# SSD output and its gate with channels on partitions in a fused two-layer decoder kernel

## The chip, the cores and the metric

The kernel runs as one program on one core of a Trainium2 chip. The metric is device time in microseconds (us) of one launch. The kernel before took 1224.19 us as the median of three runs (1223.19 to 1224.21). The engines are named as in the profile: PE is TensorE (matrix products; PEld its weight loads), DVE is VectorE, ACT is ScalarE, POOL is GpSimd, SP is SyncE, which here only issues transfers.

## What is computed

Two layers over a sequence of 256 tokens of width 2048. Layer 0 is a Mamba-2 mixer, layer 1 a dilated attention that the change doesn't touch. Cut to what matters here, with 8 groups of 8 heads of 64 channels each:

```python
proj = h @ in_w                          # 2048 -> z (4096), x/B/C (6144), dt (64)
z, xBC, dt = split(proj)
xs, Bm, Cm = split(silu(conv(xBC)))      # xs 4096, Bm and Cm 8 x 128
acum  = cumsum(dt * A)                   # per head, over the 256 tokens
decay = exp(acum[l] - acum[s])           # causal
y  = (Cm @ Bm.T * decay) @ (xs * dt)     # per head; the kernel goes in blocks of 128 tokens
y  = y + xs * D_skip
y  = y * silu(z)
y  = y * rsqrt(mean(y**2 over the 512 channels of a group) + eps) * norm_g
x  = layer_norm(alpha * x + (1 + gate) * (y @ out_w))
```

Tokens 128 to 255 take a part from the first 128 tokens through a state (`po` in the kernel: Cm times the state), scaled by exp(acum), and each block has its own part (`py`).

## The kernel before

**Products in two parts.** Every weight piece of 128x1024 f32 is loaded by SP's queue, then split: ACT copies it to a rounded type (`whi`, L100), DVE subtracts to get the rest (`wlo`, L102). A product is the sum of hi x hi, lo x hi and hi x lo, so each piece costs one ACT pass, one DVE pass and three passes on PE. A product of one group can be made with the channels on partitions (`cm_quad`: the weight is stationary, 12 matmuls of 128x256 for each 128 rows of the contraction) or with tokens on partitions (`tm_chunk`: the activations are stationary, 6 matmuls of 128x512).

**Order.** Instructions are placed on each engine by a scheduler that goes by modelled times; `issue_after` pins one instruction behind another, and `background` pops jobs from a list (columns of the adaptive gates, 128x2048 on DVE, L317) at a rate of so many for each piece. Each engine then works its list strictly in order.

**The mixer's loop.** For each group g the kernel makes B and C, xs and z of the next group while it works on this one. `scores` makes Cm x Bm. `stage1` makes the decay matrices `seg` on ACT and DVE (from `cbc`, the cumulative sums, loaded by broadcast), transposes xs to tokens on partitions (L776), and makes `xd` (times dt), the product with D (into y, L781, DVE) and `xo`. `stage2` makes `po` (one 128x512 matmul, L798), `py` (32 matmuls of 64x64, L809, whose halves go to different halves of the output partitions), adds, multiplies by silu(z), and takes sums of squares with ACT's accumulator (L812). y has tokens on partitions, so a root is one number for each partition. `stage3` scales by the root (ACT, L820).

**The output projection.** `y_tiles(g)` turns y around: eight transposes on PE (L864), and for each of four channel tiles one ACT pass (hi, L868) and one DVE pass (lo, L869), both of 128x256 from PSUM. y(0) is turned during the last z product (z of group 7), y(1) to y(7) during the first of four column groups of the output projection (`wout`, n = 0 to 3, 16 pieces each), two pieces for each y. Column group n is closed by `residual` (DVE), which takes the gate's row by a broadcast.

## Time and profile before

| what | value |
|---|---|
| median of three runs | 1224.19 us (1223.19 to 1224.21) |
| the profiled execution's own time | 1223.81 us |
| its span | 1222.0 us |
| mean granted TensorE clock | 0.999 of full speed |
| busy: PE, DVE, ACT | 1208.8, 1019.6, 703.9 us |
| stages touched by the change | the mixer's loop, about 180 to 511 us, and the first column group of the output projection, up to about 562 us |

Busy times count what an engine executes. Matmuls overlap in PE's pipeline, so a matmul of 128x512 is shown with about 392 ns though one is started about every 227 ns; how often something starts is what a row's place in time, or a run of many in the chain of waits, shows. DVE instructions overlap a little in the same way: the row's duration is longer than the time to the next start.

### The profile page before, as it was taken

To read this page: it belongs to the slowest core of one execution; us is meant where nothing else is said; L and a number is where in the kernel's file an instruction comes from. 1 tells how busy PE (TensorE), PEld (TensorE's weight loads), DVE (VectorE), ACT (ScalarE), POOL (GpSimd) and SP (SyncE) were. 2 spreads that over 40 slices of the span, in tenths; PEclk is the share of its full clock that TensorE was granted. 3 is DMA by queue.
4 is the path that set the end of the run, shared out by engine and by line. 5 is a ranking of instruction groups with operands and counts; after the bars stand their busy time and mean duration, and the time that the engine had idled before them with its cause. 6 is when DMAs were issued, how large, how long until landed. Compare 5 with 4: busy or idle time off the path is not lost.

```text
span 1222.0 us, 19072 instructions
## 1 busy us (share of the span) xinstructions
PE 1208.8 (99%) x7244; PEld 1039.5 (85%) x7244; DVE 1019.6 (83%) x1450; ACT 703.9 (58%) x1057; POOL 3.9 (0%) x8
## 2 busy tenths in 40 slices
...
GB/s 374 421 421 423 422 264 239 259 327 224 230 190 194 182 173 207 226 327 334 370 317 298 211 203 342 350 344 379 385 376 280 281 261 174 113 193 160 193 260 69
DMA packets 81372, 335.94 MB, mean 275 GB/s; under 512 B 9200, under 2 KB 9984, under 8 KB 68480
## 3 DMA queue, kind: packets, MB, share of 16 engines
...
q0 software_dynamic: 576, 1.05, 0.6%
...
q14 instruction: 35, 0.29, 0.1%
q10 hardware_dynamic: 208, 0.08, 0.0%
...
## 4 chain that ended last, share of the span: by engine, by line
PE 77%; DVE 13%; ACT 5%; DMA 3%; issue 2%; DVEq 0%; ACTq 0%
PE acc L224 25%; PE acc L190 21%; PE acc L193 11%; DVE wlo L102 4%; DVE araw L317 4%; PE acc L233 3%; PE acc L234 3%; PE acc L232 3%; DMA raw<-in_win 3%; ACT whi L100 2%; DVE cacc L391 2%; PE acc L151 1%; PE acc L153 1%; PE acc L152 1%; PE py L809 1%
## 5 line engine op out<-in xcount | busy, mean ns | idle before, releaser
L100 ACT ACTIVATE whi<-raw 128x1024 fp32r<-128x1024 f32 x389 | 408.2, 1057 | 329.5 <-PE acc L190 107.1
L102 DVE TENSOR_TENSOR wlo<-raw,whi 128x1024 fp32r<-128x1024 f32 x389 | 470.2, 1221 | 128.3 <-ACT whi L100 121.1
L190 PE MATMUL acc<-actT,whi 128*128 128x512 f32 x1280 | 401.7, 394 | 0.5 <-DVE xs L202 0.5
L193 PEld LDWEIGHTS acc<-actT,wlo 128*128 128x128 f32 x1280 | 239.6, 188 | 52.3 <-DVE wlo L102 0.7
L193 PE MATMUL acc<-actT,wlo 128*128 128x256 f32 x1280 | 255.2, 281 | 0.3 <-DVE wlo L102 0.3
L317 DVE SCALAR_TENSOR_TENSOR araw<-araw,cb__72 128x2048 f32<-128x2048 f32 x95 | 217.0, 2284 | 3.2 <-DMA araw<-in_ada 3.0
L190 PEld LDWEIGHTS acc<-actT,whi 128*128 128x128 f32 x1280 | 195.0, 188 | 1.7 <-DVE xs L202 0.9
L224 PE MATMUL acc<-whi,actT 128*128 128x512 f32 x560 | 144.5, 392 | 0.5 <-ACT whi L100 0.5
L224 PEld LDWEIGHTS acc<-whi,actT 128*128 128x128 f32 x560 | 104.2, 188 | 22.0 <-ACT whi L100 0.9
L233 PE MATMUL acc<-wlo,actT 128*128 128x512 f32 x272 | 106.8, 393 | 2.2 <-DVE wlo L102 2.1
L232 PE MATMUL acc<-whi,actT 128*128 128x512 f32 x272 | 105.0, 394 | 0.2 <-ACT sz L664 0.2
L151 PE MATMUL acc<-actT,whi 128*128 128x256 f32 x372 | 103.5, 281 | 1.0 <-ACT sz L664 0.5
L224 PE MATMUL acc<-wlo,actT 128*128 128x512 f32 x384 | 103.6, 391 | 0.0
L153 PE MATMUL acc<-actT,wlo 128*128 128x256 f32 x372 | 101.9, 281 | 1.5 <-DVE wlo L102 1.5
L152 PE MATMUL acc<-actT,whi 128*128 128x256 f32 x372 | 103.0, 279 | 0.0
L234 PE MATMUL acc<-whi,actT 128*128 128x512 f32 x256 | 100.0, 391 | 0.0
L224 PEld LDWEIGHTS acc<-wlo,actT 128*128 128x128 f32 x384 | 71.7, 188 | 14.4
L151 PEld LDWEIGHTS acc<-actT,whi 128*128 128x128 f32 x372 | 69.6, 188 | 2.6 <-ACT sz L664 0.9
L153 PEld LDWEIGHTS acc<-actT,wlo 128*128 128x128 f32 x372 | 68.9, 188 | 2.3 <-DVE wlo L102 2.3
L152 PEld LDWEIGHTS acc<-actT,whi 128*128 128x128 f32 x372 | 70.6, 190 | 0.2
L233 PEld LDWEIGHTS acc<-wlo,actT 128*128 128x128 f32 x272 | 51.1, 188 | 13.8 <-DVE wlo L102 3.7
L232 PEld LDWEIGHTS acc<-whi,actT 128*128 128x128 f32 x272 | 50.9, 188 | 10.5 <-ACT sz L664 0.6
...
## 6 DMA issues: line engine op xcount, KB each, us to landing
...
raw<-in_win SPq DMA_DIRECT2D x109, 512.0 KB, 6.0
raw<-in_wout SPq DMA_DIRECT2D x64, 512.0 KB, 5.7
raw<-in_wbin SPq DMA_DIRECT2D x64, 512.0 KB, 4.1
raw<-in_wxs SPq DMA_DIRECT2D x48, 512.0 KB, 4.5
raw<-in_wv SPq DMA_DIRECT2D x48, 512.0 KB, 6.7
raw<-in_wk SPq DMA_DIRECT2D x48, 512.0 KB, 7.6
cbc<-cumd SPq DMA_DIRECT2D x16, 512.0 KB, 5.1
```

The costliest lines, as they stand in the source:

```text
L100: copied.append(S.activation(hi, raw, AF.Copy))
L102: latest.append(V.tensor_tensor(lo, raw, hi.bitcast(F32), op=ALU.subtract))
L151: T.matmul(o, hi[:, k, c_], ahi[:, kt, :], start=first, stop=False, skip_group_check=True)
L152: T.matmul(o, hi[:, k, c_], alo[:, kt, :], start=False, stop=False, skip_group_check=True)
L153: T.matmul(o, lo[:, k, c_], ahi[:, kt, :], start=False, stop=kt == k1 - 1, skip_group_check=True)
L190: T.matmul(ps[n], hi[:, k, n * P:n * P + P], both(kt), start=kt == 0, stop=False, skip_group_check=True)
L193: T.matmul(ps[n][:, 0, :], lo[:, k, n * P:n * P + P], high(kt), start=False, stop=kt == KT - 1, skip_group_check=True)
L224: T.matmul(ps[b], a_(kt)[:, b * P:b * P + P], w_[:, k, :], start=a_ is ahi and w_ is hi and kt == k0, stop=w_ is lo and kt == k1 - 1)
L232: T.matmul(o, h_, hi[:, k, :], start=kt == k0, stop=False, skip_group_check=part)
L233: T.matmul(o, h_, lo[:, k, :], start=False, stop=False, skip_group_check=part)
L234: end = T.matmul(o, l_, hi[:, k, :], start=False, stop=kt == k1 - 1, skip_group_check=part)
L317: return V.scalar_tensor_tensor(raw, raw, 1.0, cb_, op0=ALU.mult, op1=ALU.mult, accum_out=mod[layer][:, ct, j:j + 1])
```

## The change

**z and y with channels on partitions.** z is now made by `cm_quad`, and y[g] holds four channel tiles of 128 channels by 256 tokens. `py` takes xd as the stationary operand and `seg` as the moving one: 16 matmuls with 64 weight columns and 128 moving columns each, the even heads to the lower and the odd heads to the upper half of the output partitions. `po` is four matmuls of 128x128.

**What a token-wise factor becomes.** A factor for each token is now a factor along a row. exp(acum) for `po` is made by four ACT passes of 64x256 (`grow`) in `stage1`. The product with D is a factor for each partition: four ACT passes of 128x256 instead of two DVE passes of 128x512. The mean of squares goes over partitions: ACT squares y (128x1024), DVE adds the four channel tiles in two instructions (128x512, 128x256), and PE multiplies the sum by a column of ones (two matmuls of one column). The roots go through DRAM: GpSimd's queue (POOL) writes them to `rootd` and loads them back as a broadcast over all partitions (128x256 for groups 0 and 1, one 128x1024 for groups 2 to 5, 128x256 each for 6 and 7).

**Turning y.** No transposes: DVE multiplies by norm_g and the root (`y_scale`, four passes of 128x256 out of SBUF), then one ACT pass and one DVE pass of 128x1024 split y (`y_split`).

**Order of the projection.** Column group 0 goes over its pieces 0 to 13 (y(1) to y(6) are scaled and split there, `stage3` of group 7 at piece 1), then column group 1 over its pieces 0 to 13 (y(7) at its piece 2), then pieces 14 and 15 of both, each followed by its `residual`. The rates of the background jobs change from (1, 2) and (1, 4) to (1, 3) and (2, 5).

```diff
             def stage1(g, cb):
-                segs = []
+                segs, grow = [], px.tile([P, 4, P], F32, name="grow", bufs=1)
...
+                    for n, rows_ in enumerate((slice(0, 64), slice(64, 128))):
+                        S.activation(grow[rows_, 2 * w:2 * w + 2, :], cbc[rows_, n:4:2, 1, :], AF.Exp)
...
-                    V.tensor_tensor(y[g][:, b, :].rearrange("p (h e) -> p h e", h=HPG), heads,
-                                    dskip[:, g * HPG:(g + 1) * HPG, None].to_broadcast([P, HPG, 64]),
-                                    op=ALU.mult)
...
+                for i in range(4):
+                    S.activation(y[g][:, i, :], xs[g][:, i, :], AF.Copy, scale=pv("dsk")[:, 4 * g + i:4 * g + i + 1])
...
-            def stage2(g, segs, xd, cb, xo):
+            def stage2(g, segs, xd, cb, xo, grow):
...
-                T.matmul(po, cb[:, 2, :], xo, start=True, stop=True)
...
-                behind = z_end[-1] if g in (0, 4, 7) else None
+                behind = z_end[-1] if g in (0,2,3,4,7) else None
+                for i in range(4):
+                    c_ = slice(i * P, i * P + P)
+                    with tc.issue_after(behind.ins) if behind is not None else ExitStack():
+                        behind = T.matmul(po[:, c_], xo[:, c_], cb[:, 2, :], start=True, stop=True)
+                xo = xo.rearrange("p (i n) -> p i n", i=4)
+                V.tensor_tensor(xo, po.rearrange("p (i n) -> p i n", i=4), grow, op=ALU.mult)
+                V.tensor_tensor(y[g][:, :, P:], xo, y[g][:, :, P:], op=ALU.add)
...
-                                T.matmul(py[t_, e_], segs[hh // 4][:, hh % 4, b, t_], xd[:, b, e_], start=True, stop=True)
+                                behind = T.matmul(py[t_, hh // 2, b * P:b * P + P], xd[:, b, 64 * h:64 * h + 64],
+                                         segs[w][:, hh, b, :], start=True, stop=True)
...
+                V.tensor_tensor(y[g], y[g], sz[g], op=ALU.mult)
+                sq = sz[g]
+                S.activation(sq, y[g], AF.Square)
+                return sq
-            def stage3(g, rs):
+            def stage3(g, sq):
-                for b in range(2):
-                    S.activation(y[g][:, b, :], y[g][:, b, :], AF.Copy, scale=rs[:, b:b + 1])
+                V.tensor_tensor(sq[:, 0:2, :], sq[:, 0:2, :], sq[:, 2:4, :], op=ALU.add)
+                sums = sq[:, 0, :]
+                V.tensor_tensor(sums, sums, sq[:, 1, :], op=ALU.add)
+                ss = (aux if g == G - 1 else aux2).tile([P, 512], F32, name="aux" if g == G - 1 else "py")[:, :2]
+                for b in range(2):
+                    T.matmul(ss[:, b:b + 1], sums[:, b * P:b * P + P], ones[:, 0:1], start=True, stop=True)
...
+                nc.gpsimd.dma_start(rootd[g * L:g * L + L].rearrange("(b p) -> p b", p=P), rsqrt(ms, "a"))
...
+            def y_scale(g):
+                if g < 2:
+                    roots[g] = p0.tile([P, L], F32, name="cacc", bufs=3)
+                    bcast(roots[g], rootd, g * L, queue=PO)
+                elif g in (2, 6):
+                    t = slots.tile([P, 4, L], F32, name=f"s{g // 6}")
+                    roots.update({g + j: t[:, j, :] for j in range(min(4, G - g))})
+                    n = min(4, G - 1 - g)
+                    bcast(t[:, :n, :].rearrange("p i l -> p (i l)"), rootd, g * L, queue=PO)
+                elif g == G - 1:
+                    bcast(roots[g], rootd, g * L, queue=PO)
+                for i in range(4):
+                    V.scalar_tensor_tensor(y[g][:, i, :], y[g][:, i, :], pv("normg")[:, 4 * g + i:4 * g + i + 1],
+                                           roots[g], op0=ALU.mult, op1=ALU.mult)
+            def y_split(g):
+                val = y[g].rearrange("p i (j r) -> p i r j", r=2)
+                hi, lo = (t.rearrange("p i (r j) -> p i r j", r=2) for t in y_to(g))
+                S.activation(hi, val, AF.Copy)
+                V.tensor_tensor(lo, val, hi.bitcast(F32), op=ALU.subtract)
             def y_tiles(g):
-                        T.transpose(pt[:, i % 2, b * P:b * P + P], y[g][:, b, i * P:i * P + P], ident)
...
-                    S.activation(hi, by_parity, AF.Copy, scale=w)
-                    V.scalar_tensor_tensor(lo, by_parity, w, hi.bitcast(F32), op0=ALU.mult, op1=ALU.subtract)
+                if g > 1:
+                    y_scale(g)
+                y_split(g)
...
         def y_ahead(q):
-            if q % 2 == 0 and q // 2 + 1 < G:
+            if q == 1:
+                with tc.high_priority():
+                    stage3(G - 1, rs)
+            if q % 2 == 0 and q // 2 + 1 < G - 1:
                 y_tiles(q // 2 + 1)
...
+        out_pieces(0, 0, KT - 2, y_ahead)
+        out_pieces(1, 0, KT - 2, lambda q: y_tiles(G - 1) if q == 2 else None)
+        drain()
...
+        for n in range(2):
+            out_pieces(n, KT - 2, KT)
+            joined(n, pss[n])
```

Three places of the order show how the scheduler lays this out. In them `s_94` to `s_101` are y(0) to y(7), `sz` the gate of a group and later its squares, `acc` an accumulator, `actT` the activations of the product (later the hi part of y), `xs` at these places the two parts of y(0), `ylo` the lo part of y(1) to y(7) in turn.

PE where the last z product ends and the output projection begins, first before, then with the change:

```order
2336 L234 MATMUL acc<-whi,actT 128x512
2337 L798 MATMUL aux<-xo,cb 128x512
2338 L809 MATMUL py<-xd,seg 64x64 x32
2339 L864 MATMUL aux<-cc,s_95 128x128 x4
2340 L224 MATMUL acc<-whi,xs 128x512 x8
2341 L224 MATMUL acc<-wlo,xs 128x512 x4
2342 L224 MATMUL acc<-whi,xs 128x512 x2
2343 L864 MATMUL aux<-cc,s_95 128x128 x2
```

```order
3108 L153 MATMUL acc<-actT,wlo 128x256
3109 L791 MATMUL aux<-cb,xo 128x128 x4
3110 L802 MATMUL py<-seg,xd 64x128 x16
3111 L228 MATMUL acc<-wlo,xs 128x512 x4
3112 L228 MATMUL acc<-whi,xs 128x512 x8
3113 L228 MATMUL acc<-wlo,xs 128x512 x4
3114 L228 MATMUL acc<-whi,actT 128x512 x4
3115 L818 MATMUL aux<-cc,sz 128x1 x2
3116 L228 MATMUL acc<-whi,ylo_6270 128x512 x4
```

The transposes are gone; the sum over partitions for group 7 (L818) now stands on PE between the twentieth matmul of the projection and the first that reads the lo part of y(1).

DVE at the same boundary, before and with the change:

```order
563 L102 TENSOR_TENSOR wlo<-raw,whi 128x1024 x2
564 L799 TENSOR_TENSOR xo<-aux,dec 128x512
565 L801 TENSOR_TENSOR s_101<-xo,s_101 128x512
566 L810 TENSOR_TENSOR s_101<-py,s_101 128x512
567 L102 TENSOR_TENSOR wlo<-raw,whi 128x1024
568 L811 TENSOR_TENSOR s_101<-s_101,sz 128x512
569 L810 TENSOR_TENSOR s_101<-py,s_101 128x512
570 L811 TENSOR_TENSOR s_101<-s_101,sz 128x512
571 L869 SCALAR_TENSOR_TENSOR ylo_5568<-aux,prm,actT 128x256 x2
```

```order
574 L794 TENSOR_TENSOR s_101<-xo,s_101 128x4x128
575 L871 SCALAR_TENSOR_TENSOR s_98<-s_98,prm,s_6350 128x256
576 L805 TENSOR_TENSOR s_101<-py,s_101 128x512 x2
577 L871 SCALAR_TENSOR_TENSOR s_98<-s_98,prm,s_6350 128x256
578 L806 TENSOR_TENSOR s_101<-s_101,sz 128x1024
579 L102 TENSOR_TENSOR wlo<-raw,whi 128x1024 x2
580 L813 TENSOR_TENSOR sz<-sz 128x512
581 L871 SCALAR_TENSOR_TENSOR s_98<-s_98,prm,s_6350 128x256
582 L815 TENSOR_TENSOR sz<-sz 128x256
583 L871 SCALAR_TENSOR_TENSOR s_99<-s_99,prm,s_6350 128x256
584 L820 TENSOR_SCALAR ms<-aux 128x2
585 L879 TENSOR_TENSOR ylo_6270<-s_95,actT 128x1024
```

With the change the scalings of y(2) to y(4) and one of y(5) stand ahead of the first lo part that the projection needs, and that lo part stands behind the mean of squares of group 7 (L820), which reads what L818 leaves.

DVE a little earlier, where the broadcast roots of groups 2 to 5 (`s_6350`, in the place of y(0)) are first read; this is new, and before there is nothing in its place:

```order
565 L102 TENSOR_TENSOR wlo<-raw,whi 128x1024 x3
566 L871 SCALAR_TENSOR_TENSOR s_96<-s_96,prm,s_6350 128x256
567 L102 TENSOR_TENSOR wlo<-raw,whi 128x1024
568 L871 SCALAR_TENSOR_TENSOR s_96<-s_96,prm,s_6350 128x256 x3
569 L102 TENSOR_TENSOR wlo<-raw,whi 128x1024
570 L871 SCALAR_TENSOR_TENSOR s_97<-s_97,prm,s_6350 128x256 x4
571 L102 TENSOR_TENSOR wlo<-raw,whi 128x1024
572 L793 TENSOR_TENSOR xo<-aux,grow 128x512
```

The first scaling of y(2) waits for that broadcast, and weight pieces of the last z product (L102) stand behind it.

155 lines of the change are left out of this document (72 added, 83 removed).

## The prediction

> **What bounds the kernel now.** First the page: engines, and the chain that ended last.
>
> ```profile
> span 1222.0 us, 19072 instructions
> PE 1208.8 (99%) x7244; PEld 1039.5 (85%) x7244; DVE 1019.6 (83%) x1450; ACT 703.9 (58%) x1057; POOL 3.9 (0%) x8
> PE 77%; DVE 13%; ACT 5%; DMA 3%; issue 2%; DVEq 0%; ACTq 0%
> ```
>
> PE is busy nearly all the time, and three quarters of the chain is its work, so a matmul that goes away is worth its time, unless another engine is just behind. Whether one is must be read by stage. The windows (busy time of PE, PEld, DVE, ACT; then granted clock, DMA share, GB/s):
>
> ```profile
> 180.00:222.00 42.00, 41.55 (x258) 36.85 (x257) 31.33 (x55) 33.46 (x55) 0.00 (x0) 1.00 0.72 250
> 222.00:301.00 79.00, 77.20 (x570) 67.05 (x569) 79.00 (x127) 58.10 (x99) 0.00 (x0) 1.00 0.75 263
> 380.00:470.00 90.00, 90.00 (x673) 77.99 (x672) 83.58 (x153) 79.62 (x145) 0.00 (x0) 1.00 0.61 198
> 470.00:511.00 41.00, 40.30 (x306) 33.06 (x304) 36.02 (x72) 32.88 (x57) 0.00 (x0) 1.00 0.54 187
> 511.00:562.00 51.00, 51.00 (x252) 41.46 (x252) 49.40 (x77) 30.47 (x50) 0.00 (x0) 1.00 0.85 314
> ```
>
> The clock is 1.00 in all of them. From 470 to 562 us, the last z product and the turning of y, DVE has 85.4 of 92 us: 6.6 us of room. That is where the change adds DVE work. In the loop before it, DVE is full from 222 to 301 us, and ACT has 79.6 of 90 us from 380 to 470.
>
> Then the pace of each kind of instruction, from runs of equals in the chain of waits (start, us, engine and line, count):
>
> ```profile
> 405.92 0.87 PE aux L776 x8
> 451.31 2.36 DVE cacc L391 x6
> 459.00 3.40 DVE wlo L102 x3
> 508.03 0.86 PE aux L798 x2
> 508.89 2.02 PE py L809 x64
> 561.67 119.72 PE acc L224 x528
> ```
>
> So PE takes 119.72/528 = 0.227 us for 512 columns (half of it, 0.113, for 256) and 0.109 for a transpose. `po` counts two passes and `py` 64, since these f32 products go through PE twice: 0.86 and 2.02 us a group, 0.84 ns a column. DVE takes 1.13 us for 128x1024 and 0.39 for a 256-wide operation with a scalar. The timeline of DVE (start, duration) gives the others, and DVE's rest in the last z product:
>
> ```profile
> 488.41 0.69 DVE L811 TENSOR_TENSOR s<-s,sz 128x512 f32<-128x512 f32 x1
> 489.02 0.42 DVE L750 TENSOR_TENSOR cb<-aux,cc 128x256 f32<-128x256 f32 x1
> 489.35 0.29 DVE L751 COPY cb<-aux 128x128 f32<-128x128 f32 x1
> 490.69 0.16 DVE L814 TENSOR_SCALAR ms<-ss 128x2 f32<-128x2 f32 x1
> 490.76 0.69 DVE L778 TENSOR_TENSOR xd<-aux,dtT 128x512 f32<-128x512 f32 x1
> 503.77 1.23 DVE L102 TENSOR_TENSOR wlo<-raw,whi 128x1024 fp32r<-128x1024 f32 x1 [0.50 <-ACT whi L100]
> 506.49 1.23 DVE L102 TENSOR_TENSOR wlo<-raw,whi 128x1024 fp32r<-128x1024 f32 x1 [1.49 <-ACT whi L100]
> 508.93 0.69 DVE L799 TENSOR_TENSOR xo<-aux,dec 128x512 f32<-128x512 f32 x1 [1.21 <-PE aux L798]
> ```
>
> From start to start: 0.61 us for 128x512, 0.33 for a plain 256-wide one, 0.07 for 128x2. In brackets stand 3.2 us in which DVE waited.
>
> **The change part by part.**
>
> z costs PE the same either way: 12 x 0.113 against 6 x 0.227 us for 128 rows of the contraction. The gate's ACT and DVE work keeps its size. Nothing here.
>
> *Transposes of y.* 64 go. Bare, by the pace above, 64 x 0.109 = 7.0 us. In the first column group they stand singly among matmuls; the timeline of PE has the first and the last of 56 of them:
>
> ```profile
> 510.83 0.66 PE L864 MATMUL aux<-cc,s 128*128 128x128 f32 x4
> 554.54 0.38 PE L864 MATMUL aux<-cc,s 128*128 128x128 f32 x2
> ```
>
> By the order of the kernel before, 54 transposes and 163 matmuls of 512 columns lie between these starts: 43.71 - 163 x 0.227 = 6.7 us, 0.124 each, 8.0 for 64. I take -7.5 (-7.0 to -8.0).
>
> *py.* Before, 64 passes of 64 columns take 2.02 us, 31 ns each, where 64 columns at 0.84 ns are 54: the two halves of the output partitions run side by side. Now 32 passes of 128 columns, 107 ns alone. Side by side in the same proportion they take 1.9 us a group (-0.15, over eight groups -1.2); perfectly, 1.7 (-2.3); one behind the other 3.4 (+11.4). Before, both halves read the same moving data and now they read different data. The rows of the second layer's halves are the nearest:
>
> ```profile
> L1162 PE MATMUL aux<-s,q x96: 221/222/271, 1028.1 to 1137.6; 128*64 128x64 f32 x96
> ```
>
> They have the same 222 ns of latency as L809's, which speaks for side by side. I take -1.2.
>
> *po.* Four matmuls of 128 columns for one of 512, same columns: +0.04 us a group for three more starts, +0.3 (0 to +0.8).
>
> *Sums over partitions.* Two one-column matmuls a group, four passes with a full weight load, 32 in all; no row has one. Between 31 ns (L809's pass) and 109 (L776's): 1.0 to 3.5 us. The load is a full one, but it can overlap; I take the middle, +2.0.
>
> *The loop, groups 0 to 6.* DVE loses two 128x512 products with D (1.22 us) and gains the two adds of the squares (0.61 + 0.39); the small rest leaves about -0.3 a group. ACT changes more. Its rows in the last z product:
>
> ```profile
> L868 ACT ACTIVATE actT<-aux,prm 128x256 fp32r<-128x256 f32 x28 | 12.3, 468 | 9.0 <-PE aux L864 9.0
> L820 ACT ACTIVATE s<-s,ay 128x512 f32<-128x512 f32 x6 | 4.0, 715 | 1.1 <-DVE ay L281 1.1
> L765 ACT ACTIVATE seg<-cbc,cumT 128x128 f32<-128x128 f32 x16 | 5.1, 387 | 0.0
> ```
>
> The product with D costs 4 x 0.47, `grow` about 4 x 0.4 to 0.47, the two scalings (2 x 0.72) go: about +1.8 us a group. From 380 to 470 us ACT has 10.4 us of room for some three groups, 3.5 each: hidden, with half the cover used up; without it, 1.8 a group. PE's own rest from 180 to 301 us is 0.45 + 1.8 = 2.3 us, which DVE's relief could take away. I take -0.5 (-2.3 to +2).
>
> *The stretch where y is finished.* I follow DVE's order from the mean of squares of group 5 to the lo part of y(1), and PE's from the sums (L818) of group 5 to the first matmul that reads that lo part; DVE cannot start before PE's sums, nor PE pass the end before DVE. DVE has 17 of 128x1024 (11 are lo parts of weights), 16 of 128x512, 32 of about 128x256, 24 of 128x2 and a copy: 17 x 1.13 + 16 x 0.61 + 32 x 0.39 + 24 x 0.07 + 0.2 = 43.4 us. PE has 192 z matmuls of 256 columns (21.8), 28 of the projection (6.3), 16 transposes (1.7), scores (0.6), two `po` and two `py` (1.7 + 3.8) and four one-column matmuls (0.4): 36.3 us, with about 1 for switching. So PE must wait 6 to 7 us somewhere in it, however early DVE's inputs come. The cause is what the rearrangement puts on DVE there: the lo parts of y cost 0.4 x 4 from PSUM before; now the scaling costs that, and the split 1.13 on top, for each y. The products with D, which left DVE, were spread over the loop.
>
> The order puts the largest part of it at the end. Behind the last z product PE has `po` and `py` (2.8 us) and 20 matmuls (4.5), then the sums of group 7. They wait for DVE's eight operations from the `po` product to the multiply by silu(z) (4.8 us), ACT's square, two lo parts and the adds: 9.4 us behind z's end at the least, 2.1 after PE is there, and the lo part of y(1) 1.3 later. With DVE already late by some 3 us, of which z's own pieces take part, I get 8.5 in all by hand. I take +7.3 (6 to 8.5). The kernel before's own rest in this stretch, 0.7 us by the window from 470 to 511, is part of that and comes off: -0.7.
>
> *The broadcast roots.* POOL's queue can load the roots of groups 2 to 5 only when y(0)'s split has freed its place; four lo parts, one scaling and a few tiny ones later, 5.3 us by DVE's pace, DVE wants them, and three weight pieces of z stand behind it. The rows of such transfers (time to landing), and of an issue on POOL:
>
> ```profile
> cbc<-cumd SPq DMA_DIRECT2D x16, 512.0 KB, 5.1
> L1350 POOL DMA_DIRECT2D out<-u x4: 996/1287/1558, 1207.2 to 1209.5; - x4
> DMA to landing us min/median/max: 4.2/8.1/8.6
> ```
>
> By the broadcast of the same size on SP, 5.1 us, the roots are just in time; with the issue of 1.3 and POOL's slowest landing of 8.6 they are 4.6 late, a lateness that goes straight into DVE's sum. I take 0 (0 to +4.6), since the nearest row is the one of the same pattern and size.
>
> *The projection behind it.* After the lo part of y(1), DVE has 1.13 us of split, 1.6 of scaling and about two weight pieces for each y, while PE has 24 matmuls (5.4 us) for it, so DVE gets ahead again. The joining of column groups 0 and 1 moves back by 28 pieces together, so the gate's row has more time. 0.
>
> Sum: -7.5 - 1.2 + 0.3 + 2.0 - 0.5 + 7.3 - 0.7 = -0.3 on the profiled 1223.81, 1223.5; the median of the runs is 0.4 above the profiled execution, so **1223.9 us**: no change that a measurement can tell (0.2%, 2.4 us, is about what one of this kernel can).
>
> [...]
>
> **Rivals.**
>
> *PE's saving shows.* If the scalings out of SBUF start every 0.33 us, as the plain 256-wide row L750 does, the 32 operations of that width give 1.9 us back; if the loop's relief takes away PE's 2.3 us of rest; and with transposes at -8.0: -0.3 - 1.9 - 1.8 - 0.5 = -4.5, or 1219.7; with sums at 1.0 and `py` at -2.3, 1217.6. I call it 1218.5. For it: L391's six run in dependent pairs, so its 0.39 may hold a wait, and DVE is full from 222 to 301 us. Against it: L869, a scaling of the same form out of PSUM, has 0.40 too, and PE's rests there come from weight pieces.
>
> *The roots come late.* The mechanism above, slower: with POOL's landing at its median of 8.1 us and the issue of 1.3 they are 4.1 late, 1228.0; with the hand count of 8.5 on the boundary, 1229.2. It decides from a landing of about 5.3 us after the split. For it: the median of POOL's rows is above; against it: those are stores at the end of the kernel, in competition with SP's.
>
> *The halves of py run one behind the other.* +12.6 against my term: 1236.5, less what DVE's lateness in the last two groups hides (1.6 each at most), about 1234. For it: different moving data in the halves. Against: the latency of L1162. [...]
>
> **Chances.** Forecast (within 0.2%) 0.37; PE's saving shows 0.35; the roots or the boundary later than I count 0.20; halves in sequence 0.08. So faster by over 0.2% 0.35, within it 0.37, slower 0.28. The forecast's own range is 1221.8 to 1226.6, the bounds of no change. The whole one reaches to the lower end of the first rival and a little past the second's hand count: 1217 to 1230.
>
> **What would show it.** `po`, `py` as grouped runs: 0.9 and 1.9 us (3.4 would be the third rival). No rows at all of L864's kind. PE's waits in the last z product and the first twenty matmuls of the projection: 6 to 8.5 us in sum, released by DVE's `wlo` and `ylo`; under 4 would be the first rival. At the first scaling of y(2), DVE waiting on a DMA by over 1 us would be the second. The scalings' pace, 0.39 or 0.33. The forecast is wrong if PE's waits in the loop grow by over 2 us (ACT's cover gone), or if the join of column groups 0 and 1 waits.

## The result

The changed kernel takes **1236.88 us** (median of six runs, 1235.23 to 1240.34) where the kernel before takes 1224.20 (1223.19 to 1225.40): a ratio of 1.0109, 95% interval 1.0092 to 1.0126. It is 12.7 us slower. The forecast was 1223.9 us with a range of 1217 to 1230; the result lies outside it, on the side that had a chance of 0.28. Among the kernels further down, one execution of burst_earlier is left out, which took 1495.92 us at a granted clock of 0.753.

The profiled execution took 1240.34 us, 3.5 more than its kernel's median, so what is read from the trace below adds up to more than 12.7 us. The first lines of the page, and the chain of waits by engine:

```profile
span 1238.5 us, 20144 instructions
PE 1210.6 (98%) x7772; PEld 1074.9 (87%) x7772; DVE 1026.3 (83%) x1450; ACT 711.5 (57%) x1056; POOL 12.5 (1%) x21
PE 73%; DVE 11%; ACT 7%; DMA 6%; issue 3%; SPq 0%; DVEq 0%; ACTq 0%
```

PE is busy 1.8 us longer than before in a span 16.5 us longer, though it has less to do, and the chain runs through ACT and DMA more often (7% and 6% against 5% and 3%). Work has left PE, and waiting has come in.

### The profile page after: what moved, and what is told of

It is laid out like the page before. It is cut to its first block, busy times and chain, and to the rows that moved or that the text cites. A ratio compares the mean times of both kernels' runs of the same rounds, so it can differ in the third digit from the quotient of the medians.

```text
span 1238.5 us, 20144 instructions
## 1 busy us (share of the span) xinstructions
PE 1210.6 (98%) x7772; PEld 1074.9 (87%) x7772; DVE 1026.3 (83%) x1450; ACT 711.5 (57%) x1056; POOL 12.5 (1%) x21
## 4 chain that ended last, share of the span: by engine, by line
PE 73%; DVE 11%; ACT 7%; DMA 6%; issue 3%; SPq 0%; DVEq 0%; ACTq 0%
PE acc L228 23%; PE acc L194 21%; PE acc L197 11%; DMA raw<-in_win 3%; DVE wlo L102 3%; DVE araw L320 3%; PE acc L153 3%; PE acc L151 3%; PE acc L152 3%; ACT whi L100 2%; DVE cacc L392 2%; DMA araw<-in_ada 2%; ACT seg L757 1%; PE py L802 1%; PE acc L238 1%
## 5 line engine op out<-in xcount | busy, mean ns | idle before, releaser
L102 DVE TENSOR_TENSOR wlo<-raw,whi 128x1024 fp32r<-128x1024 f32 x389 | 470.2, 1221 | 135.9 <-ACT whi L100 130.5
L197 PEld LDWEIGHTS acc<-actT,wlo 128*128 128x128 f32 x1280 | 239.5, 188 | 54.5 <-DVE wlo L102 2.3
L197 PE MATMUL acc<-actT,wlo 128*128 128x256 f32 x1280 | 254.8, 280 | 1.5 <-DVE wlo L102 1.3
L153 PE MATMUL acc<-actT,wlo 128*128 128x256 f32 x884 | 242.1, 279 | 7.9 <-DVE wlo L102 7.9
L151 PE MATMUL acc<-actT,whi 128*128 128x256 f32 x884 | 245.4, 280 | 1.3 <-ACT whi L100 0.7
L152 PE MATMUL acc<-actT,whi 128*128 128x256 f32 x884 | 244.6, 278 | 0.0
L194 PEld LDWEIGHTS acc<-actT,whi 128*128 128x128 f32 x1280 | 194.8, 188 | 0.6
L153 PEld LDWEIGHTS acc<-actT,wlo 128*128 128x128 f32 x884 | 164.8, 189 | 10.1 <-DVE wlo L102 9.9
L151 PEld LDWEIGHTS acc<-actT,whi 128*128 128x128 f32 x884 | 166.9, 189 | 2.9 <-ACT whi L100 0.9
L152 PEld LDWEIGHTS acc<-actT,whi 128*128 128x128 f32 x884 | 166.9, 189 | 0.2 <-issue 0.2
L228 PE MATMUL acc<-whi,actT 128*128 128x512 f32 x560 | 144.4, 392 | 0.5 <-ACT whi L100 0.5
L228 PEld LDWEIGHTS acc<-whi,actT 128*128 128x128 f32 x560 | 105.1, 189 | 23.0 <-ACT whi L100 0.9
L228 PE MATMUL acc<-wlo,actT 128*128 128x512 f32 x384 | 104.1, 393 | 0.0
L228 PEld LDWEIGHTS acc<-wlo,actT 128*128 128x128 f32 x384 | 72.7, 189 | 16.0
L228 PE MATMUL acc<-whi,ylo 128*128 128x512 f32 x208 | 57.4, 399 | 1.4 <-DVE ylo L879 1.4
L757 ACT ACTIVATE seg<-cbc,cumT 128x128 f32<-128x128 f32 x128 | 40.9, 388 | 5.1 <-PE py L802 3.4
```

Of the source, the lines that this page charges most:

```text
L102: latest.append(V.tensor_tensor(lo, raw, hi.bitcast(F32), op=ALU.subtract))
L151: T.matmul(o, hi[:, k, c_], ahi[:, kt, :], start=first, stop=False, skip_group_check=True)
L152: T.matmul(o, hi[:, k, c_], alo[:, kt, :], start=False, stop=False, skip_group_check=True)
L153: end = T.matmul(o, lo[:, k, c_], ahi[:, kt, :], start=False, stop=kt == k1 - 1, skip_group_check=True)
L194: T.matmul(ps[n], hi[:, k, n * P:n * P + P], both(kt), start=kt == 0, stop=False, skip_group_check=True)
L197: T.matmul(ps[n][:, 0, :], lo[:, k, n * P:n * P + P], high(kt), start=False, stop=kt == KT - 1, skip_group_check=True)
```

## The profile after, and where the time went

I went through PE's list in the trace from 180 us to the first matmul of layer 1 and gave each matmul its steady pace (0.227 us for 512 columns, 0.113 for 256, 59 ns for a pass of the new `py`, 31 for one of the old, and so on); what lies between two starts beyond that is counted as lost. The marks are starts of state products (`po`).

| stretch of PE's list | before: work, lost (us) | after: work, lost (us) |
|---|---|---|
| 180 us to the sixth state product (452.5 / 459.7 us) | 265.0, 7.6 | 264.7, 14.9 |
| sixth to eighth state product (507.9 / 519.6 us) | 52.7, 2.7 | 54.0, 6.0 |
| eighth to the first matmul of layer 1 (692.9 / 708.5 us) | 181.6, 3.5 | 175.9, 12.9 |
| sum | 499.3, 13.8 | 494.6, 33.8 |

So 4.7 us of work are saved and 20.0 us more are lost: +15.3 at the end of the mixer (15.5 by the marks; the table is good to some 0.2 us). Layer 1 adds another 0.9 to the profiled span's matmuls and is not followed here. The loss stands at three places: the loop (+7.3), the last z product (+3.3) and the start of the output projection (+9.4).

**The loop.** The windows (busy time of PE, PEld, DVE, ACT, POOL; then granted clock, DMA share, GB/s), in three of the stretches that were shown of before:

```profile
222.00:301.00 79.00, 74.47 (x582) 69.95 (x581) 75.95 (x119) 58.17 (x98) 0.87 (x1) 0.98 0.71 251
380.00:470.00 90.00, 90.00 (x679) 82.83 (x678) 81.47 (x150) 78.70 (x140) 2.17 (x3) 1.00 0.71 173
...
511.00:562.00 51.00, 44.01 (x242) 37.24 (x241) 46.38 (x70) 23.03 (x23) 2.54 (x4) 0.90 0.84 236
```

From 380 to 470 us, where I feared for ACT's room, PE still has 90 of 90. The loss in the loop is earlier: from 222 to 301 us PE is busy for 74.47 us, before for 77.20, and the granted clock has fallen under 1. The other one is at the boundary, 511 to 562 us, where PE had 51 of 51 and now has 44.01, at a clock of 0.90. PE's longest waits, summed over the run (us in total, times, longest):

```profile
PE acc L153 <- DVE wlo L102: 7.9, 9, 3.2
PE aux L818 <- DVE sz L815: 5.6, 1, 5.6
```

The 3.2 us are one wait, in the z product of the second group. The row of PE's timeline that ends it:

```profile
232.24 0.38 PE L153 MATMUL acc<-actT,wlo 128*128 128x256 f32 x1 [3.18 <-DVE wlo L102]
```

And windows of 4 us around it:

```profile
230.00:234.00 4.00, 1.76 (x14) 1.76 (x15) 4.00 (x7) 3.45 (x5) 0.00 (x0) 0.95 0.18 40
234.00:238.00 4.00, 4.00 (x24) 4.00 (x24) 4.00 (x7) 1.82 (x3) 0.00 (x0) 0.62 0.87 261
238.00:242.00 4.00, 4.00 (x37) 4.00 (x37) 4.00 (x4) 1.27 (x3) 0.00 (x0) 1.00 0.89 323
```

DMA has little under way there (18% of its time), and DVE is full: the weights' split is late. Behind the rest the granted clock is 0.62 in a window in which PE is busy throughout and starts 24 matmuls, where the next window has 37. So the rest costs twice: 3.2 us of waiting, and 13 matmuls of 0.113, some 1.5 us, at half speed.

**The boundary.** The chain of waits from the last state product on (start, us, what):

```profile
519.81 0.89 PE aux L791 x8
520.70 1.90 PE py L802 x32
522.60 2.49 PE acc L228 x10
525.09 3.08 ACT actT L878 x3
...
530.29 1.22 DVE wlo L102
...
532.99 1.00 PE aux L818 x4
534.17 1.14 DVE ylo L879
535.36 9.68 PE acc L228 x30
```

`po` takes 0.89 us and `py` 1.90, as forecast, and after them PE has twenty matmuls to make (the chain holds ten of them) before it stands, from 527.4 to 533.0 us. The last row takes 9.68 us for 30 matmuls, 6.8 at the steady pace: here too PE comes back at half clock, as the windows show:

```profile
530.00:535.00 5.00, 0.98 (x4) 0.93 (x4) 4.23 (x8) 2.14 (x3) 0.00 (x0) 0.56 0.63 206
535.00:540.00 5.00, 4.64 (x11) 3.67 (x12) 4.76 (x9) 1.06 (x1) 0.55 (x1) 0.50 0.98 388
```

Why DVE is late there, the windows of exactly the two stretches that the prediction summed say: DVE's, from the mean of squares of group 5 to the first lo part of y(1), and PE's, from the sums of group 5 to the first matmul that reads it.

```profile
486.80:534.10 47.30, 38.78 (x321) 35.48 (x319) 42.91 (x92) 33.02 (x52) 2.57 (x5) 0.96 0.56 149
485.40:535.40 50.00, 40.22 (x335) 36.92 (x333) 45.34 (x94) 34.42 (x56) 3.12 (x5) 0.95 0.58 157
```

DVE is busy for 42.91 us; the prediction had counted 43.4. But the stretch takes 47.3, so DVE stood still for 4.4 us, and the two hand-overs at its ends take 1.4 and 1.3 us more. Nearly half of the 4.4 us, 2.05, is one wait. What it was for is shown by a row each of the timelines of DVE and ACT (start, duration; in brackets the time idle before and its releaser):

```profile
522.72 1.23 DVE L102 TENSOR_TENSOR wlo<-raw,whi 128x1024 fp32r<-128x1024 f32 x1 [2.05 <-ACT whi L100]
521.63 1.06 ACT L100 ACTIVATE whi<-raw 128x1024 fp32r<-128x1024 f32 x1 [5.28 <-DMA raw<-in_wout]
```

and one of the waits of SP's queue:

```profile
SPq L90 <- DVE at L282: 11.2, 1, 11.2
```

DVE waits for ACT's hi part, and ACT for a weight piece. SP's queue had waited 11.2 us for a buffer, until 506.2 us, since ACT made no hi part from 487.7 to 503.9 us, when decays, `grow`, the square of y and products with D stood in its list (and 2.2 us of waiting); before, that gap was from 480.2 to 491.0. But that is not the whole way to the late piece. By its issue and landing in the trace it was issued at 511.81 us, when DVE had freed one more buffer, behind the scalings of y(0) and y(1) and the split of y(0), and it took 9.7 us to land, at 521.55. ACT had been free for it since 516.35. While it was under way, from 512.1 to 521.8 us, one of the new stores of roots was too, and weight pieces land late beside these in the whole run. The pages have the loads of `in_win` (KB each, median us from issue to landing), before and after:

```profile
raw<-in_win SPq DMA_DIRECT2D x109, 512.0 KB, 6.0
```

```profile
raw<-in_win SPq DMA_DIRECT2D x109, 512.0 KB, 9.4
```

In the change's trace from 180 to 600 us, the 28 pieces issued between the issue and the landing of such a store took 7.8 to 13.2 us to land, 10.2 in the median; the 71 issued neither then nor in the 10 us before a store took 5.0, and the kernel before, which has no such stores, has 4.9. With 5.0 the late piece would have landed at 516.8, an estimate from these medians, and nearly all of ACT's 5.28 us of waiting would be gone.

## Experiments

Three theories went into them. **A**: the half clock behind PE's rests costs the time. **B**: `grow`, new on ACT, makes the weights' hi parts late in the loop. **C**: DVE's work and order at the boundary set its end. Each table row below is one kernel; "lag" is how much later than in the kernel before PE starts, in the profiled execution, the sixth and the eighth state product and layer 1 (in us, good to some 0.2); "lost" is as above, for the three stretches. One execution's lag is a rough number: at the sixth product it lies between 5.2 and 9.0 us in five kernels that are the same up to there (the change, keep_clock, late_scales, late_both, first_tiles; mean 7.0).

| kernel | ratio to before, 95% | lag: sixth, eighth, layer 1 | lost in the three stretches |
|---|---|---|---|
| (the change) | 1.0109 (1.0092 to 1.0126) | 7.2, 11.8, 15.5 | 14.9, 6.0, 12.9 |
| keep_clock | 1.0112 (1.0097 to 1.0127) | 9.0, 13.5, 14.4 | 16.0, 6.0, 3.3 |
| no_grow | 1.0076 (1.0061 to 1.0091) | 4.1, 7.2, 10.6 | 11.8, 4.5, 12.5 |
| late_scales | 1.0127 (1.0107 to 1.0147) | 7.4, 11.9, 13.3 | 15.0, 6.0, 10.5 |
| late_both | 1.0139 (1.0108 to 1.0169) | 5.9, 10.7, 16.2 | 13.6, 6.3, 14.7 |
| act_free | 1.0105 (1.0090 to 1.0120) | 5.1, 8.6, 10.9 | 12.6, 4.9, 11.4 |
| y_on_pool | 1.0221 (1.0206 to 1.0236) | 8.0, 15.1, 26.9 | 15.0, 10.4, 19.1 |
| join_before | 0.9996 (0.9987 to 1.0006) | -0.1, -0.1, -0.1 | 7.1, 2.7, 3.5 |
| d_on_pool | 1.0109 (1.0094 to 1.0124) | 7.0, 10.7, 14.5 | 14.6, 5.1, 12.9 |
| grow_behind | 1.0079 (1.0064 to 1.0094) | 3.0, 8.9, 10.6 | 9.9, 7.3, 10.9 |
| grow_d_behind | 1.0115 (1.0100 to 1.0130) | 3.3, 12.7, 14.2 | 9.7, 12.7, 8.9 |
| behind_scales | 1.0088 (1.0073 to 1.0103) | 0.7, 9.3, 10.2 | 8.9, 11.8, 8.3 |
| behind_scales_clock | 1.0123 (1.0104 to 1.0142) | 1.6, 9.8, 14.4 | 9.0, 11.4, 5.2 |
| behind_plain | 1.0086 (1.0071 to 1.0101) | 2.2, 7.2, 10.7 | 9.7, 6.5, 12.7 |
| behind_d_pool | 1.0092 (1.0072 to 1.0112) | 4.5, 8.0, 13.3 | 11.1, 4.9, 14.5 |
| burst_earlier | 1.0088 (1.0071 to 1.0105) | 0.5, 8.3, 9.4 | 8.3, 10.0, 9.4 |
| burst_later | 1.0096 (1.0079 to 1.0112) | 3.0, 9.4, 11.7 | 9.7, 8.2, 11.0 |
| first_tiles | 1.0099 (1.0082 to 1.0116) | 5.2, 9.8, 11.9 | 12.4, 6.0, 11.4 |
| first_tiles_behind | 1.0075 (1.0060 to 1.0090) | 2.3, 7.6, 7.4 | 9.6, 6.8, 9.0 |

### The join of the column groups alone

The kernel before, with only the new order of the output projection's pieces and the joint end of column groups 0 and 1:

```diff
-        for n in range(4):
-            ps = tm_chunk(wout[n], ..., rate=(1, 4) if n else (1, 2), pre={0: y_ahead, ...}.get(n), ...)
+        out_pieces(0, 0, KT - 2, y_ahead)
+        out_pieces(1, 0, KT - 2)
+        ...
+        for n in range(2):
+            out_pieces(n, KT - 2, KT)
+            joined(n, pss[n])
```

> The kernel before with one part of the change alone: column groups 0 and 1 over pieces 0 to 13 each, then 14 and 15 of both, with the changed rates of background jobs. Theory (the order of the projection costs and brings nothing): within 1 us of the kernel before, 1223 to 1225. Rival (it hides some of the loss, or adds to it: y(7) early, residuals together): more than 2 us away from it.

0.9996: nothing, as the prediction had it. The 12.7 us belong to the turned y and what it needs.

### The half clock

Thirty matmuls whose result nobody reads are put where PE rests at the boundary (and the last sums stand one piece later):

```diff
+                if g == G - 1:
+                    last, idle = w_end[-1], aux.tile([P, 512], F32, name="aux")
+                    for _ in range(30):
+                        with tc.issue_after(last.ins):
+                            last = T.matmul(idle, y_first[0][:, 0, :P], ..., start=True, stop=True)
...
-            if q == 1:
+            if q == 2:
```

> The changed kernel, with 30 more matmuls of 512 columns (into a bank that nobody reads) right ahead of the sums of group 7, where PE waited 5.6 us. 30 x 0.227 = 6.8 us of work, 6.0 of them in time in which PE stood still. Theory A (a still PE loses half its clock for 10 us behind the wait, 13 matmuls at 0.43 instead of 0.227 = 2.7 us): the clock stays at 1.00 from 530 to 545 us and the kernel is 2 to 3 us faster than the changed one, about 1234. Rival (the low clock comes from something else than the rest of PE): the clock stays at 0.5 there, and the time is 1237 or up to 4 us more.

Its windows around the wait in the loop, which it leaves alone, and at the boundary:

```profile
222.00:242.00 20.00, 16.19 (x116) 15.80 (x115) 17.11 (x25) 13.28 (x22) 0.00 (x0) 0.83 0.58 198
525.00:545.00 20.00, 19.65 (x89) 15.89 (x88) 17.43 (x30) 8.80 (x9) 0.55 (x1) 1.00 0.89 306
```

At the boundary the clock stays at 1.00, and the lag grows by 0.9 us from the eighth state product to layer 1, where the change's grows by 3.7: theory A holds in this stage, for 2.8 us of this one execution. The median doesn't show it: 1237.63 us where about 1234 was expected. In the profiled execution the clock in the loop was lower than in the change's own from 222 to 242 us (0.83 against 0.91), though nothing had been changed there. How long it stays low differs between executions of equal work: 3.4 us behind the change's rest of 3.2 us, and some 6.8 behind keep_clock's of 3.8, by the means of these windows. At half speed the 3.4 us more are 1.7 us of work, and the rest is 0.6 longer: an estimate of 2.3 us from these figures, near the gain looked for. As a gain in time theory A is not shown.

### `grow`: its time or its place

First `grow` is left out, and the state product is multiplied by part of `seg` in its place; then besides that the product with D goes back to DVE:

```diff
-                    for n, rows_ in enumerate((slice(0, 64), slice(64, 128))):
-                        S.activation(grow[rows_, 2 * w:2 * w + 2, :], cbc[rows_, n:4:2, 1, :], AF.Exp)
...
-                return segs, xd, cb, xo, grow
+                return segs, xd, cb, xo, segs[0][:, :, 0, :]
```

> The changed kernel without the four exponentials of 64x256 a group on ACT (grow); the product that used them takes a part of seg in their place, so the factor exp(acum) of the second block is left out. Theory B (the new waits of PE in the loop, 3.2 us at 232 with a half clock behind it, 1.4 at 272, 1.2 at 327, come from ACT, which the new exponentials make late with the hi parts of the weights): 4 to 6 us faster than the changed kernel, 1231 to 1233, and the wait at 232 under 1.2 us. Rival (they come from the order of DVE's and PE's work for z, not from ACT's load): within 1.5 us of 1237, the wait at 232 still 2 us or more.

> The changed kernel without grow (as in no_grow: exp(acum) of the second block is left out) and with the product with D on DVE (four of 128x256 a group) in place of ACT: ACT loses all that the change gave it in the loop, DVE gets 4 x 0.39 = 1.6 us a group back. Theory B (ACT's added load makes the loop late): the time up to the last group's state product, 11.6 us behind the kernel before in the changed kernel and 7.2 in no_grow, falls to 3 or less; total 1228 to 1230. Rival (what no_grow left is DVE's and the order's, not ACT's): 6 to 8 us stay, total 1232 to 1235.

Without `grow` the lag at the sixth state product is 4.1 us instead of 7.2, and the median 4.2 us lower. To free ACT of the product with D as well gains nothing on top: 1237.44 us, by the ratios 3.5 more than without `grow` alone, and more than either theory expected. DVE, which then makes that product, may be the reason; no run shows it. The product with D on GpSimd, with `grow` back in its place:

```diff
-                    S.activation(y[g][:, i, :], xs[g][:, i, :], AF.Copy, scale=pv("dsk")[:, 4 * g + i:4 * g + i + 1])
+                    nc.gpsimd.tensor_scalar(y[g][:, i, :], xs[g][:, i, :], pv("dsk")[...], None, op0=ALU.mult)
```

> The changed kernel with the product with D (four of 128x256 a group) on GpSimd in place of ACT: ACT loses 1.9 us a group, DVE gets nothing. Theory B: as for no_grow, which took 1.6 us a group from ACT, 3 to 5 us faster than the changed kernel, 1232 to 1234. Rival (only grow counts, since it stands between the hi parts of the weights and seg, while the product with D comes where ACT has time): within 1.5 us of 1237.

The same time as the change, though ACT has 11 us less to do over the run (700.4 us of work for 711.5). So it isn't ACT's load as a sum. A kernel that leaves nothing out and moves only the place of `grow` in the program text settles it:

```diff
-                    for n, rows_ in enumerate((slice(0, 64), slice(64, 128))):
-                        S.activation(grow[rows_, 2 * w:2 * w + 2, :], cbc[rows_, n:4:2, 1, :], AF.Exp)
+                    cbcs.append(cbc)
...
             def stage2(g, segs, xd, cb, xo, cbcs):
+                grow = px.tile([P, 4, P], F32, name="grow", bufs=1)
+                for w, cbc in enumerate(cbcs):
+                    for n, rows_ in enumerate((slice(0, 64), slice(64, 128))):
+                        S.activation(grow[rows_, 2 * w:2 * w + 2, :], cbc[rows_, n:4:2, 1, :], AF.Exp)
```

> The four grow exponentials of a group stand in ScalarE's program behind the group's decays and behind two or three more hi parts of the weights, instead of between the decays; nothing is left out. Theory B1 (their place costs: they hold back the hi parts that TensorE's next z product needs): like the run without grow, z's first product waits under 1.6 us instead of 3.4, no half clock there, lag behind the kernel before at the first state product about 0 instead of +3.5, and 1231 to 1234 us. Rival B2 (their time costs, 2.2 us of ScalarE per group, wherever they stand): the lag at the first state product stays +3 and the time 1235 to 1238 us.

ACT's timeline in the second group, of the change:

```profile
216.34 1.05 ACT L100 ACTIVATE whi<-raw 128x1024 fp32r<-128x1024 f32 x1
217.29 1.05 ACT L759 ACTIVATE seg<-seg 128x1024 f32<-128x1024 f32 x1
...
221.47 1.04 ACT L759 ACTIVATE seg<-seg 128x1024 f32<-128x1024 f32 x1
222.54 0.41 ACT L761 ACTIVATE grow<-cbc 64x256 f32<-64x256 f32 x1
222.98 2.96 ACT L100 ACTIVATE whi<-raw 128x1024 fp32r<-128x1024 f32 x3
```

DVE's, at the same time:

```profile
218.56 1.22 DVE L762 TENSOR_TENSOR seg<-seg,cb 128x1024 f32<-128x1024 f32 x1
222.55 1.23 DVE L762 TENSOR_TENSOR seg<-seg,cb 128x1024 f32<-128x1024 f32 x1 [2.77 <-ACT seg L759]
228.21 2.84 DVE L392 SCALAR_TENSOR_TENSOR cacc<-xs,prm,cacc 128x255 f32<-128x255 f32 x7
```

From 217.4 to 222.98 us ACT makes no hi part; three `grow` operations and the second half of the decays lie there. DVE has no lo part to make meanwhile and stands for 2.77 us. Then its own block for the group comes due (xd, xo and the convolution, 225.2 to 231.0 us), and PE runs dry in it. ACT's timeline in grow_behind:

```profile
219.16 1.05 ACT L100 ACTIVATE whi<-raw 128x1024 fp32r<-128x1024 f32 x1
222.16 1.05 ACT L100 ACTIVATE whi<-raw 128x1024 fp32r<-128x1024 f32 x1
...
225.01 1.71 ACT L788 ACTIVATE grow<-cbc 64x256 f32<-64x256 f32 x4
```

The hi parts stand between the decays, as in the kernel before, and from 219 us to that block DVE makes three lo parts, where in the change it makes one. Of PE's waits of this kind, over the run,

```profile
PE acc L153 <- DVE wlo L102: 5.6, 8, 1.5
```

the longest is 1.5 us instead of 3.2 (that one is in the last z product; at this place it is 1.2), and the window that was at 0.62 is at full clock with 38 matmuls:

```profile
234.00:238.00 4.00, 4.00 (x38) 4.00 (x37) 4.00 (x7) 3.56 (x5) 0.00 (x0) 1.00 0.73 204
```

1234.76 us, 1.0079 of before; the lag at the first state product is 1.0 us instead of 3.8, at the sixth 3.0 instead of 7.2. That is level with the kernel without `grow` (1.0076), so the 1.7 us of ACT's time per group cost nothing measurable, and the place costs all that these runs can tell. The new order even gives ACT more to do: it has 40 table loads (`ACT_TABLE_LOAD`, 1.28 us each) where the change has 32, and 722.3 us of work in the run where the change has 711.5. What these eight loads cost further on, no kernel tells. Three pairs of kernels differ only by this move (the change and grow_behind, first_tiles and first_tiles_behind, late_scales and behind_plain): by their ratios 3.7, 2.9 and 5.0 us. Theory B is right in this sharper form.

### The boundary: order on DVE

The scalings of y(2) to y(6) are held behind the first lo part (late_scales), and then the last one-column sums are held behind five pieces of the projection too (late_both):

```diff
-                    V.scalar_tensor_tensor(y[g][:, i, :], ..., roots[g], op0=ALU.mult, op1=ALU.mult)
+                    with tc.issue_after(y_lo[1].ins) if g > 1 else ExitStack():
+                        V.scalar_tensor_tensor(y[g][:, i, :], ..., roots[g], op0=ALU.mult, op1=ALU.mult)
```

> The changed kernel with the scalings of y(2) to y(6) pinned behind the lo part of y(1) on DVE: 14 operations, 5.5 us by 0.39 each, leave the place ahead of the boundary. Theory C (DVE's work sets the wait at the boundary): the sums of group 7 and the lo part of y(1) come 4 to 5 us earlier, no half clock; 1229 to 1232. Rival (the wait there is the chain silu, multiply, square, sums on ACT and a late weight piece, not DVE's load): under 2 us gained, 1235 or more.

> As late_scales, and the two one-column matmuls of group 7 moved on PE from ahead of the first use of y(1)'s lo part to five pieces behind it (their input is kept in a place that stays free). Theory C: little over late_scales, 0 to 2 us, since the lo part itself is then what PE waits for; 1228 to 1231. Rival (the sums of group 7 are what holds PE): 5 us or more better than late_scales.

With the scalings late the wait at the sums falls from 5.6 to 1.7 us and the lag from the eighth product to layer 1 grows by 1.4 instead of 3.7 us, but the median is no better (1238.41 us, late_both 1240.15). With the sums late too, PE waits as long at the next thing, by its waits in late_both:

```profile
PE acc L228 <- DVE ylo L886: 5.5, 1, 5.5
```

The timelines of DVE and ACT there:

```profile
521.68 1.23 DVE L102 TENSOR_TENSOR wlo<-raw,whi 128x1024 fp32r<-128x1024 f32 x1 [4.39 <-ACT whi L100]
520.59 1.06 ACT L100 ACTIVATE whi<-raw 128x1024 fp32r<-128x1024 f32 x1 [5.46 <-DMA raw<-in_wout]
```

DVE, relieved, now stands 4.39 us for the late weight piece. That piece, too, is under way beside a store of roots (510.8 to 520.6 us). So neither the sums nor the scalings hold the end alone, and theory C, which says that they do, falls.

The root's multiplication on GpSimd (norm_g goes into the split, four passes of 128x256 each on ACT and DVE):

```diff
-                for i in range(4):
-                    V.scalar_tensor_tensor(y[g][:, i, :], y[g][:, i, :], pv("normg")[...], roots[g], ...)
+                PO.tensor_tensor(y[g], y[g], roots[g][:, None, :].to_broadcast([P, 4, L]), op=ALU.mult)
```

> The changed kernel with the multiplication of y by the root on GpSimd (one 128x1024 a group) in place of DVE (four of 128x256), and norm_g put into the split (ACT and DVE four passes of 128x256 each, as before the change). DVE loses 8.6 us (22 x 0.39) ahead of the first use of y(1)'s lo part and gets 1 back. Theory C (DVE's work sets the boundary): the waits of PE there fall from 7.0 us to under 2, no half clock; 1228 to 1231, unless a GpSimd operation takes over 5 us each (then y(2) to y(6) come late one after the other, up to +5). Rival (the late weight piece and the chain of silu, square and sums set it): 5 us of waits or more stay, 1235 or more.

1251.76 us, by the ratios 14 us slower than the change, and not a clean test, since POOL's queue carries the roots too. Its two groups of instructions (busy us, mean ns; idle before):

```profile
L870 POOL TENSOR_TENSOR s<-s,s 128x1024 f32<-128x1024 f32 x6 | 15.9, 2665 | 15.9 <-DMA s<-rootd 15.8
L870 POOL TENSOR_TENSOR s<-s,cacc 128x1024 f32<-128x1024 f32 x2 | 4.9, 2447 | 11.9 <-DMA cacc<-rootd 11.9
```

It takes 2.4 to 2.7 us for what DVE does in four operations of 0.39, and waits 27.7 us for the transfers of its own queue.

### The boundary: the burst on ACT, and both causes together

The product with D is also written behind the hi parts (grow_d_behind), then the scalings late as well (behind_scales), then thirty idle matmuls besides (behind_scales_clock). The added edit is:

```diff
             def stage2(g, segs, xd, cb, xo, cbcs):
...
+                for i in range(4):
+                    S.activation(y[g][:, i, :], xs[g][:, i, :], AF.Copy, scale=pv("dsk")[:, 4 * g + i:4 * g + i + 1])
                 po = aux.tile([P, 512], F32, name="aux")
```

> Besides the grow exponentials, the D product of a group (xs times D, four 128x256 operations of ScalarE) is also written behind the weights' hi parts of the z stage, just ahead of the state product. If ScalarE's burst of decays, grow and D product in the last group is what made SyncE's weight loads 11 us late before the boundary (theory: burst holds raw buffers), the wait of SyncE there shrinks, no hi part of wout comes late, and TensorE waits under 4 us instead of 5.8 + 1.7 at the last one-column sums: 1228 to 1232 us. Rival (the order on VectorE alone sets the boundary): 5 to 6 us of waiting remain there and the time is that of the run with grow alone moved, plus or minus 1 us.

> grow and the D product behind the hi parts, and the scalings of groups 2 to 6 by their roots behind the first lo part that the second column group needs. If the two causes add (loop: about -4 us; boundary: about -2.3 us and a shorter half clock), 1228 to 1231 us. If the scalings only move the wait to the next weight piece, no faster than the run before it in this list.

> The same with 30 matmuls of no use ahead of the last one-column sums, which fill TensorE's rest there (about 6.8 us at full speed). If the half clock behind that rest still cost its 2.7 us, 1226 to 1229 us; if the rest is too short to lower the clock any more, or the filling is longer than the wait, the same time as without it or up to 2 us more. All three causes named so far out of the way, what is left against the kernel before (1224) is the work that stands between the last mean of squares and the first lo part on VectorE, which would be 2 to 5 us.

None came as expected: 1238.87, 1236.05 and 1239.60 us. SP's longest wait there is 11.4 us in grow_d_behind, no shorter than the change's 11.2, so moving the product with D out of the burst does not shorten it. The projection's start loses less (8.9, 8.3 and 5.2 us), but the last z product loses as much more: 12.7, 11.8 and 11.4 where grow_behind loses 7.3. The idle matmuls cost more than they save: 6.8 us of work for 3.1 less lost, since in behind_scales the clock is at 1.00 from 520 to 535 us without them. In grow_d_behind PE now rests in the last z product, at the sums of group 6:

```profile
PE py L822 <- DVE sz L819: 3.2, 1, 3.2
```

The wait has changed its place. Four more kernels on grow_behind with late scalings: as it is (behind_plain), with the D product on GpSimd (behind_d_pool), and with the last group's burst one piece of the z product earlier or later:

```diff
             def last_scores(q):
-                if q == 2:
+                if q == 1:
```

(burst_later has 3 there.)

> grow behind the hi parts (the D product left where the change has it) and the scalings of groups 2 to 6 behind the first lo part of the second column group. If the two gains add (grow's place about -3 us by the medians, the scalings about -2.3 us in the stage), 1229 to 1232 us and a lag behind the kernel before, from the last state product to the layer's end, of under 2 us. If the scalings' move only hands the wait on, 1233 to 1236 us as with grow alone.

> The kernel behind_plain with the D product on GpSimd, which takes four 128x256 operations of about 0.5 us per group off ScalarE and gives them to an engine that is 1% busy. Theory L (ScalarE's load holds the stage from the sixth group on, 99% busy there): SyncE's loads come earlier, the wait of TensorE at the last one-column sums falls under 2 us, and the time is 2 to 4 us under behind_plain's. Rival P (the order holds it, not the load): within 1 us of behind_plain.

> behind_plain with the last group's scores, decays and D product written one piece of the z product earlier (ahead of piece 1 instead of 2). Theory P2 (the burst's place sets the boundary): its end and with it the last squares come about 3 us earlier, and less waiting at the last one-column sums, against more at the z product's pieces; time 2 us under behind_plain's or more. Rival: the waits only change places, within 1.5 us.

> behind_plain with the same burst one piece later. By theory P2 the weights' hi parts of one more z piece come ahead of the burst, SyncE's loads for the output product start some 3 us earlier, and the decays come 3 us later: the pair products of the last group then wait. If the late weight piece is what costs, 1 to 3 us less than behind_plain; if the last decays and squares are, 2 to 3 us more. If neither, within 1.5 us.

All four come to 1235.1 to 1236.7 us, within the spread of any one of them. ACT's load (theory L) and the burst's place (theory P2) both fail as the one cause: burst_earlier takes 3.3 us off the projection's start against behind_plain and puts 3.5 on the last z product.

### More work for PE ahead of y(1)

The pieces of column groups 0 and 1 that read only y(0) come first, so PE has 48 instead of 24 matmuls before it needs y(1); alone, and on grow_behind:

```diff
-        out_pieces(0, 0, KT - 2, y_ahead)
-        out_pieces(1, 0, KT - 2, lambda q: y_tiles(G - 1) if q == 2 else None)
+        out_pieces(0, 0, 2, y_ahead)
+        out_pieces(1, 0, 2)
+        out_pieces(0, 2, KT - 2, y_ahead)
+        out_pieces(1, 2, KT - 2, lambda q: y_tiles(G - 1) if q == 2 else None)
```

> The change with the output product's pieces in another order: the two pieces of column group 0 that read y's group 0, then the two of column group 1 that read it too, then the rest of group 0 and of group 1 as before. TensorE has 48 matmuls (10.9 us at 0.227) instead of 24 before it needs the first lo part of y's group 1. Theory W (TensorE had no other work): its waits of 5.8 + 1.7 us at the last one-column sums and the first lo part fall under 2 us together, the clock there is not halved (2.7 us), and the time falls by 5 to 9 us, to 1228 to 1232. Rival S (weights hold the stage: late pieces, SyncE waiting for buffers): the two pieces come no earlier, the wait stands at their hi or lo parts instead, and the time stays within 2 us of 1236.9.

> The same order of pieces, with the grow exponentials behind the hi parts (the run that gained about 3 us in the loop). If both causes are what they seem, they add: 1224 to 1229 us, level with the kernel before or up to 5 us over it. By rival S 1233 to 1236 us.

PE's wait at the last sums in first_tiles,

```profile
PE aux L818 <- DVE sz L815: 2.6, 1, 2.6
```

in first_tiles_behind,

```profile
PE aux L822 <- DVE sz L819: 1.2, 1, 1.2
```

and the window of the boundary in the latter:

```profile
520.00:540.00 20.00, 18.78 (x84) 15.20 (x83) 19.29 (x30) 11.59 (x13) 0.55 (x1) 1.00 0.92 346
```

The wait goes as expected, from the change's 5.6 us to 2.6 and on to 1.2; no matmul waits for `ylo` any more, and in the second kernel the clock stays full. But the medians are 1236.91 and 1234.51 us, where 1228 to 1232 and 1224 to 1229 were expected. In the profiled executions the stretch behind the eighth product gains 1.5 and 1.9 us against the change and grow_behind; what else PE loses there is not followed. By the medians the first gains nothing. Theory W is right on the mechanism and wrong on the price; rival S fits the times better.

No version came near the kernel before: the best of them, first_tiles_behind, is 0.75% slower (0.60 to 0.90).

## Why the prediction was wrong, point by point

**Right.** The transposes are gone, with no row of that kind left, and `po` and `py` take 0.89 and 1.90 us a group, as forecast (0.9 and 1.9): the halves run side by side though their moving data differ, 59 ns a pass, and the third rival falls. For `py` the exact size is partly luck: 32 passes of 107 ns in the proportion of 31 to 54 ns make 2.0 us, not 1.9. DVE's work in the stretch is 42.9 us for 43.4. PE's list saves 4.7 us at steady pace; the sum of the four terms for PE was -6.4. The difference is mostly the sums over partitions, whose four passes take some 0.36 us a group from start to start, 2.9 in all for the +2.0 taken, and the transposes, which the table counts at their bare 7.0 us for the 7.5 taken. The roots of groups 2 to 5 come in time. Among the transfers of POOL's queue (KB each, us from issue to landing) theirs is

```profile
s<-rootd POOLq DMA_DIRECT2D x1, 512.0 KB, 4.6
```

and the first scaling that reads them, in DVE's timeline, shows no wait: the second rival's condition wasn't met. It was close, with the broadcast issued at 510.37 us and landed some 0.2 us before that scaling. The row under it has four scalings in a run.

```profile
515.14 0.48 DVE L871 SCALAR_TENSOR_TENSOR s<-s,prm,s 128x256 f32<-128x256 f32 x1
519.00 1.67 DVE L871 SCALAR_TENSOR_TENSOR s<-s,prm,s 128x256 f32<-128x256 f32 x4
```

The join costs nothing (join_before). The scalings start every 0.40 us, not every 0.33 (1.67 less one duration of 0.48, over three), so the first rival had no ground.

**Wrong, step one: "The loop, groups 0 to 6", -0.5 (-2.3 to +2).** Measured +7.3 us of lost time up to the sixth state product. The sign that the prediction had named for this came true: PE's idle time in that stretch grows from 2.3 to 6.4 us, by more than 2. The step asked whether ACT has room, in sums over windows, and it has (78.70 of 90 us from 380 to 470). It didn't ask what stands behind `grow` in ACT's list. There stand the hi parts of the weights that PE needs next; with 1.7 us more ahead of them DVE first stood without input and then had its lo parts behind its own block, one piece came 3 us late, and the rest at the z product drew the half clock after it. grow_behind takes 4 us of lag away without leaving any of the work out. What remains, 0.5 to 3.3 us over the kernels with `grow` moved (the product with D left on ACT), is of the size of one execution's spread. In grow_behind it comes behind the second state product (0.3 us there, 3.0 at the sixth), and its cause stays open.

**Wrong, step two: "The stretch where y is finished", +7.3 (6 to 8.5).** The mechanism was right as far as it goes, and so was DVE's work. The stretch is 50.0 us long on PE, against 36.3 of work and 1 for switching: 12.7 lost. The term took DVE as busy without a break; 4.4 us of standing still and 2.7 of hand-overs were left out, less 0.5 of work counted too much. Of the standing still, 2.05 us are the wait for the late weight piece. The prediction named the engines' sums and not the ring of SP, ACT and DVE that has to turn at the same time; and it priced the way of the roots through DRAM only by when the broadcast lands, with nothing for the weights' loads beside the stores, which landed in 10.2 us for 5.0 otherwise.

**Wrong by omission: the clock.** The prediction read 1.00 in every window of before and went on with it. Behind the two new rests the clock is halved, some 1.5 us in the loop and 2.7 at the boundary of the profiled execution. The change's six executions have mean clocks of 0.992 to 0.997 over the whole run, and the lowest goes with one of the two longest (0.992, 1240.16 us), the highest with the shortest (0.997, 1235.23); but 0.994 stands beside 1236.88 twice and 1240.34 once, so the clock alone does not set the time.

With the first two terms as measured (+7.3 and 12.7) and the clock at the boundary (+2.7), the prediction's own sum, -0.3 + 7.8 + 5.4 + 2.7, comes to +15.6 against the profiled execution's +16.5.

**What stays open.** With `grow` behind the hi parts some 9 us remain by the medians, spread over the last z product and the projection's start. Eight kernels moved or removed work there; the waits changed place each time, and the sum lost in both stretches stayed between 15.8 and 21.6 us in the change and in those with `grow` moved and no idle matmuls (6.2 before). I read that as the ring of weight buffers turning too slowly there, with ACT and DVE both needed for each piece. It is argued, not shown: a kernel with more than the six buffers was not run. A rival stands beside it, and no run separates the two: all these kernels write the roots to DRAM with eight small stores, and in each of them the weight pieces issued while one is under way take 9.8 to 11.8 us to land in the median, where the others take 5.0 to 5.7. The kernel before and join_before have no such stores and 4.9 and 4.6 us. No kernel leaves the stores out or writes the roots in another form. The first rest in the loop, at 229 us, is none of theirs, since the first store is issued at 297.
